# Four reorderings in a two-layer transformer step: query loads, weight splits and the first steps of a layer change places

## The chip, the cores and the metric

The kernel runs on one core of one Trainium2 chip. Its five engines work side by side, each through its own instructions in order: PE (matmuls), DVE, ACT, POOL and SP, which here only issues transfers. The metric is the time of one execution in microseconds (us), as the median of several runs.

## The reference

A step of a streaming encoder: 1024 prompt tokens and 64 sample tokens (1088 rows of 1024) go through two layers. All arithmetic is in float32.

```python
# layer 0: 8 latent heads (keys and values from a compressed latent, with a rotary part)
#          and 8 band heads (own chunk and 8 before, learned bias) side by side
y = concat([o_a, o_b]) @ w_out
x = LN(alpha * x + y);  x = LN(alpha * x + sqrelu_mlp(x))
# layer 1: 16 stick-breaking heads
w = where(mask, exp(log_sigmoid(z) + tail), 0);  o = w @ v
x = LN(alpha * x + o @ w_out);  x = LN(alpha * x + sqrelu_mlp(x))
```

Keys, values and latents of the new tokens are outputs too.

## The kernel before, in words

**Split products.** Each float32 operand is split into a high part (ACT, L148) and a low part (DVE, L149); a product is three matmuls, high x high, low x high, high x low (L153, L154, L155). So every weight, every activation and every softmax tile passes through ACT and DVE before PE can use it. `weight` (L179) loads a weight by SP and splits it.

**Order.** The program is written as steps, and a scheduler that models the engines puts each engine's instructions in an order. The kernel steers it with `after` and `paced`: a mark says "this instruction is to be ordered after that one". A mark makes no wait on the chip; it only moves an instruction in its engine's queue. Waits come from data and from buffers that are reused. SP can have at most eight transfers outstanding: the ninth waits for the first.

**Layer 0.** (1) `latents` projects the latents. (2) The queries (L466 `nope`, L474 `rotate`): query weights `u..` times the normed latents; the results are written to DRAM as `qm_d` and `qr_d` through four `raw` buffers, with constants `qc` beside them. (3) Band heads in four pairs (`heads64`), then (4) latent heads in four pairs (`proj_mla`, L934). While a pair is attended (`attend`: scores, softmax on DVE, ACT and POOL, transposes `t`, products `pv` with the values, result `o` written to `oT_d`), the steps that project the next pair are strewn between its units by `paced`. `attend` gives back a mark for each unit. In front of the latent heads stand the values of all latent heads (`vals`, 11 blocks) and the first pair's keys; the keys' shared rotary half is copied to a second set of buffers (`k0H`.., L930 to L932), and a part of the values too (`V`, L970). Each pair loads its queries from `qm_d` and `qr_d` (L943, L944).

**The end of each layer's mixer.** In the last pair, `out_early` (L1055) loads the eight blocks of the output weights (`in_w_out`), splits them (`wo_2`, `wo_3`, `wo_4` and so on are raw, high and low) and starts the output projection for the tokens that are already complete (EARLY), with PE free between the units. `out_proj` (L1117) does the rest, with an operand load (`oT_d`) and a residual load (`in_x` or `x_d`) for each block of tokens, and the layer norm.

**Layer 1.** After the MLP of layer 0, `finish` normalises each block of tokens, and `to_x` (L202) transposes and splits it as x for layer 1. `heads64` makes steps "k, q, v" each in three chunks of tokens (CHUNKS); for the first pair they run in the order k0 k1 k2 q0 q1 q2 v0 v1 v2.

Tile names in the rows below end in a number, which differs between two builds for the same tile.

Of the kernel before, what the change touches and what calls it, by code (L numbers as in the profile page):

```python
# [7 lines left out]
F32 = mybir.dt.float32  # L8
# [5 lines left out]
P = 128  # L14
# [37 lines left out]
def pieces(n):  # L52
    if n <= 512:
# [8 lines left out]
        [(0, 0), (1, 1), (0, 1), (1, 2), (0, 4), (1, 3), (0, 2), (0, 3), (1, 0)]]  # L62

# [56 lines left out]
class Net:  # L120
# [26 lines left out]
    def split(self, H, L, src, engine=None):  # L147
        self.nc.scalar.activation(H, src, AF.Copy)  # L148
        (engine or self.nc.vector).tensor_tensor(L, src, H.bitcast(F32), op=ALU.subtract)  # L149
# [29 lines left out]
    def weight(self, src, shape, mark=None):  # L179
# [10 lines left out]
        self.split(tiles[1], tiles[2], tiles[0])  # L190
# [11 lines left out]
    def to_x(self, y, rows):  # L202

        n = sum(r[1] for r in rows)
        for h in range(2):
            tp = self.ps("t", (P, 4, P))
            for j in range(4):
                c = (4 * h + j) * P
                self.transpose(tp[:, j, :n], y[:n, c : c + P])
            for t0, m, r in rows:  # L210
                s = (slice(None), slice(None), slice(t0, t0 + m))
                self.split(self.xH.tiles[h][s], self.xL.tiles[h][s], tp[:, :, r : r + m])

# [240 lines left out]
    def queries(self, qn, uw):  # L454
# [46 lines left out]
        late = None  # L501
        for m in range(4):
            for c in range(3):
                i = nope(m, c)
                late = late or i
            if m == 0:
                first = self.weight(io["w_bk"][0], [P, KD, P], late)
        for c0, n in CHUNKS:
            qc = self.tl(up, [ROPE, 384], "qc", 2)
            self.after(nc.sync.dma_start(qc[:, :n], io["qconst"][:, c0 : c0 + n]), late)  # L510
# [48 lines left out]
    def heads64(self, cp, bp, tiles, pair, w, cacheT, cache_v, outs, out0, cache_outs=(None, None), first=None, sooner=None):  # L559
# [57 lines left out]
        steps = [lambda a=a: step(*a) for a in ((kind, c0, n) for kind in "kqv" for c0, n in CHUNKS)]  # L617
# [197 lines left out]
    def even_mixer(self):  # L815
# [105 lines left out]
        self.paced(vals[:8], marks[1:])  # L921
# [8 lines left out]
        for e, half in ((0, slice(64, 128)), (1, slice(0, 64))):  # L930
            for a, b in zip(*(k[e] for k in ksets)):
                nc.sync.dma_start(b[half].bitcast(F32), a[half].bitcast(F32))  # L932

# [33 lines left out]
        self.paced(steps + vals[8:], None)  # L967

        Vs.append(self.tl(vb, [P, 11, 2, P], "V", 1, F32R))
        nc.sync.dma_start(Vs[1].bitcast(F32), Vs[0][:, :, 6:].bitcast(F32))  # L970
        for pair in range(4):
# [9 lines left out]
            marks = self.attend(cp, heads, row, 0)  # L981
            if pair == 3:
                ws, ys, steps = self.out_early(0, io["w_out0"], io["x"])
# [804 lines left out]
```

## Time and profile before

| | |
|---|---|
| median of 3 runs | 2856.91 us (2856.05 to 2858.45) |
| profiled execution | 2852.04 us |
| its span (first to last instruction) | 2850.3 us |
| mean granted clock of PE | 0.985 |
| idle time of PE in the span | 118.1 us |

A wait is named by the engine, the tile and line that wait, and the engine, tile and line waited for. The granted clock is that of PE, as a share of full speed. The DMA share is the mean busy share of the 16 DMA engines. Rows of SP ("SPq") are the issue of a transfer, not its run.

### The profile page before, as it was taken

How to read it: one execution, taken by the hardware profiler on the slowest of the kernel's cores; microseconds unless marked ns; L12 is line 12 of the kernel's file. 1: busy time of each engine (PE TensorE's matmuls, PEld its weight loads, DVE VectorE, ACT ScalarE, POOL GpSimd, SP SyncE). 2: the span in 40 equal slices, each digit the busy share in tenths (PEclk: the TensorE clock that was granted, in tenths of full speed). 3: DMA queues.
4: the chain of work that ended last, by engine and by line, in shares of the span. 5: the costliest groups of instructions: out<-in, count | busy, mean ns of one | idle time of the engine just before them, and what ended most of it. 6: DMA issues, size and time to landing. Idle time of an engine off the chain costs nothing.

```text
span 2850.3 us, 46910 instructions
## 1 busy us (share of the span) xinstructions
PE 2732.2 (96%) x16907; PEld 2497.7 (88%) x16907; DVE 2154.3 (76%) x3827; ACT 1511.9 (53%) x3104; POOL 767.9 (27%) x888
## 2 busy tenths in 40 slices
PE   8999996999999999999999999999899999999998
PEld 7989995887899998888789999998789999977886
DVE  4336675884877777999967888878777777789998
ACT  4226674883555555433257777777545555543331
POOL 3113332652300002222443433434330000122235
PEclk9999998999999999999999999999999999999999
DMA  6162234334234357443321111112252443654432
GB/s 196 33 188 67 70 99 105 75 109 118 93 132 152 129 167 262 122 153 118 123 82 60 50 52 50 61 52 69 87 160 90 153 146 133 232 179 130 157 120 78
DMA packets 228680, 331.47 MB, mean 116 GB/s; under 512 B 44736, under 2 KB 161120, under 8 KB 228448
## 3 DMA queue, kind: packets, MB, share of 16 engines
q1 hardware_dynamic: 228448, 328.48, 36.4%
q8 instruction: 134, 2.20, 0.3%
q14 instruction: 98, 0.80, 0.1%
HBM read 214.49 MB, written 109.99 MB: 114 GB/s over the span
## 4 chain that ended last, share of the span: by engine, by line
PE 74%; DVE 10%; ACT 5%; DMA 4%; issue 4%; POOL 2%; SPq 1%; DVEq 0%; ACTq 0%; POOLq 0%
PE d L153 9%; PE d L154 8%; PE d L155 8%; PE t L153 5%; PE t L155 5%; PE t L154 5%; PE s L153 5%; PE s L155 5%; PE s L154 5%; PE t L171 4%; PE s L642 3%; PE pv L776 2%; PE pv L774 2%; PE pv L155 2%; PE pv L153 2%
## 5 line engine op out<-in xcount | busy, mean ns | idle before, releaser
L710 POOL TENSOR_TENSOR G<-G,S 128x384 f32<-128x384 f32 (+4 forms) x200 | 204.1, 1024 | 346.3 <-DVE S L707 121.4
L153 PE MATMUL d<-xH,wH 128*128 128x384 f32 (+1 forms) x784 | 262.5, 335 | 3.0 <-ACT qS L599 2.2
L155 PE MATMUL d<-xH,wL 128*128 128x384 f32 (+1 forms) x784 | 262.3, 335 | 0.0
L154 PE MATMUL d<-xL,wH 128*128 128x384 f32 (+1 forms) x784 | 260.2, 332 | 0.0
L149 DVE TENSOR_TENSOR wtL<-t,wtH 128x512 fp32r<-128x512 f32 (+2 forms) x328 | 197.4, 619 | 54.4 <-ACT wtH L148 43.5
L148 ACT ACTIVATE wtH<-t 128x512 fp32r<-128x512 f32 (+2 forms) x328 | 170.1, 545 | 55.1 <-PE pv L774 24.3
L148 ACT ACTIVATE wo<-wo 128x1024 fp32r<-128x1024 f32 (+4 forms) x109 | 95.8, 887 | 156.7 <-DMA wo<-a_d 24.8
L774 PE MATMUL pv<-wtH,V 128*128 128x256 f32 (+1 forms) x624 | 159.7, 282 | 9.7 <-DVE o L738 6.6
L649 POOL TENSOR_TENSOR R<-R,inv 128x640 f32<-128x640 f32 (+6 forms) x100 | 116.1, 1173 | 186.9 <-DVE inv L648 132.4
L776 PE MATMUL pv<-wtL,V 128*128 128x256 f32 (+1 forms) x624 | 154.9, 290 | 9.7 <-DVE wtL L149 9.6
L707 DVE TENSOR_TENSOR_SCAN S<-S,own 128x513 f32<-128x513 f32 (+3 forms) x144 | 145.9, 1023 | 10.8 <-ACT S L700 9.0
L153 PEld LDWEIGHTS d<-xH,wH 128*128 128x128 f32 x784 | 148.2, 189 | 6.6 <-ACT qS L599 3.2
L155 PEld LDWEIGHTS d<-xH,wL 128*128 128x128 f32 x784 | 148.1, 189 | 1.2
L154 PEld LDWEIGHTS d<-xL,wH 128*128 128x128 f32 x784 | 148.1, 189 | 1.1
L776 PEld LDWEIGHTS pv<-wtL,V 128*128 128x128 f32 x624 | 121.0, 194 | 13.9 <-DVE wtL L149 12.6
L774 PEld LDWEIGHTS pv<-wtH,V 128*128 128x128 f32 x624 | 120.6, 193 | 14.0 <-DVE o L738 5.7
L171 PE MATMUL t<-ident,G 128*128 128x128 f32 x600 | 105.1, 281 | 15.9 <-POOL S L698 8.1
L149 DVE TENSOR_TENSOR wo<-wo,wo 128x1024 fp32r<-128x1024 f32 (+4 forms) x80 | 94.2, 1184 | 24.4 <-ACT wo L148 24.0
L642 PE MATMUL s<-kS,qH 128*128 128x384 f32 (+3 forms) x288 | 105.8, 369 | 3.6 <-DVE mx L665 1.8
L700 ACT ACTIVATE S<-s 128x384 f32<-128x384 f32 (+4 forms) x200 | 98.9, 494 | 17.6 <-PE s L642 15.4
L701 ACT ACTIVATE G<-s 128x384 f32<-128x384 f32 (+4 forms) x200 | 99.7, 499 | 0.1
L642 PE MATMUL s<-kS,qL 128*128 128x384 f32 (+3 forms) x288 | 96.8, 339 | 0.0
(1819 smaller groups left out, 9819.3 us busy)
## 6 DMA issues: line engine op xcount, KB each, us to landing
wo<-a_d SPq DMA_DIRECT2D x59, 512.0 KB, 3.9
wo<-in_w_dn SPq DMA_DIRECT2D x30, 512.0 KB, 5.7
a_d<-wo SPq DMA_DIRECT2D x27, 544.0 KB, 3.7
a_d<-sl SPq DMA_DIRECT2D x23, 544.0 KB, 3.4
sl<-in_w_up SPq DMA_DIRECT2D x22, 512.0 KB, 4.6
sl<-a_d SPq DMA_DIRECT2D x21, 512.0 KB, 3.9
sl<-in_w_dn SPq DMA_DIRECT2D x19, 512.0 KB, 5.0
xs<-a_d SPq DMA_DIRECT2D x19, 512.0 KB, 3.8
```

The costliest lines, as they stand in the source:

```text
L148: self.nc.scalar.activation(H, src, AF.Copy)
L149: (engine or self.nc.vector).tensor_tensor(L, src, H.bitcast(F32), op=ALU.subtract)
L153: i = mm(out, aH, bH, start=first, stop=False)
L154: mm(out, aH, bL, start=False, stop=False)
L155: mm(out, aL, bH, start=False, stop=last)
L171: return self.nc.tensor.transpose(out, in_, self.ident[:n, :n])
L642: self.nc.tensor.matmul(ps[:, :n], q, k, start=i == 0, stop=i == len(passes) - 1)
L649: nc.gpsimd.tensor_tensor(R[:, :nk], R[:, :nk], inv.to_broadcast([P, nk]), op=ALU.mult)
L707: nc.vector.tensor_tensor_scan(s[r], s[r], own, carry, op0=ALU.mult, op1=ALU.max)
L710: nc.gpsimd.tensor_tensor(G[:, :n], G[:, :n], S[:, 1 : n + 1], op=ALU.mult)
L774: mm(out, v, wH[:, s : s + n], start=bi == 0 and s == 0, stop=False)
L776: mm(out, v, wL[:, s - n : s], start=False, stop=bi == len(banks) - 1 and j == bank[-1][0])
```

## The change

It has four parts.

1. *Queries.* In the query phase, the load of the first band key weight is marked after the fifth `nope` block and its split after the ninth; the constants after the third; what followed `late` follows the tenth.
2. *Latent heads.* The copies of the keys and values move behind marks of the first latent pair's units; six instead of eight value blocks are strewn through the last band pair, the others and the first pair's key steps are marked after its last unit.
3. *Weight splits.* In `out_early` each split gets a mark of a unit of the last pair, by the table WEIGHTS. In `out_proj` the residual of the first block of tokens takes another buffer, and the layer norm's constants are loaded after the first product.
4. *Start of layer 1.* The first pair's steps run k0 q0 k1 q1 k2 q2 v0 v1 v2, and the transposes of the last two blocks of tokens are marked after steps 1 and 2.

```diff
+WEIGHTS = [[0, 1, 1, 2, 2, 3, 3, 5], [0, 0, 1, 1, 2, 2, 2, 5]]
...
-    def split(self, H, L, src, engine=None):
-        self.nc.scalar.activation(H, src, AF.Copy)
+    def split(self, H, L, src, engine=None, mark=None):
+        self.after(self.nc.scalar.activation(H, src, AF.Copy), mark)
...
-        self.split(tiles[1], tiles[2], tiles[0])
+        self.split(tiles[1], tiles[2], tiles[0], mark=ready)
...
-        late = None
-        for m in range(4):
-            for c in range(3):
-                i = nope(m, c)
-                late = late or i
-            if m == 0:
-                first = self.weight(io["w_bk"][0], [P, KD, P], late)
+        marks = [nope(m, c) for m in range(4) for c in range(3)]
+        late = marks[9]
+        first = self.weight(io["w_bk"][0], [P, KD, P], marks[4], marks[8])
         for c0, n in CHUNKS:
             qc = self.tl(up, [ROPE, 384], "qc", 2)
-            self.after(nc.sync.dma_start(qc[:, :n], io["qconst"][:, c0 : c0 + n]), late)
+            self.after(nc.sync.dma_start(qc[:, :n], io["qconst"][:, c0 : c0 + n]), marks[2])
...
-        self.paced(vals[:8], marks[1:])
+        self.paced(vals[:6], marks[1:])
...
-        self.paced(steps + vals[8:], None)
-        Vs.append(self.tl(vb, [P, 11, 2, P], "V", 1, F32R))
-        nc.sync.dma_start(Vs[1].bitcast(F32), Vs[0][:, :, 6:].bitcast(F32))
+        self.paced(steps + vals[6:], marks[-1:], 0)
+        def copies(marks):
+            for e, half in ((0, slice(64, 128)), (1, slice(0, 64))):
+                for a, b in zip(*(k[e] for k in ksets)):
+                    self.after(nc.sync.dma_start(b[half].bitcast(F32), a[half].bitcast(F32)), marks[1 + e])
+            Vs.append(self.tl(vb, [P, 11, 2, P], "V", 1, F32R))
+            self.after(nc.sync.dma_start(Vs[1].bitcast(F32), Vs[0][:, :, 6:].bitcast(F32)), marks[7])
...
+            if pair == 0:
+                copies(marks)
...
-                                io["cache_skT"], io["cache_sv"], {"k": io["o_skT"], "v": io["o_svT"]}, 0)
+                                io["cache_skT"], io["cache_sv"], {"k": io["o_skT"], "v": io["o_svT"]}, 0,
+                                order=None if pair else (0, 3, 1, 4, 2, 5, 6, 7, 8))
         score, V, steps = proj(0)
-        self.paced(steps, None)
+        firsts = [st() for st in steps]
+        for t, i in zip(self.turned[-2:], (1, 2)):
+            self.after(t, firsts[i])
...
-        for k in blocks + [self.late]:
+        for k, i in zip(blocks + [self.late], WEIGHTS[layer]):
...
-            self.split(*ws[k], raw)
+            self.split(*ws[k], raw, mark=marks[i])
...
-        loads, ops = {}, {order[0]: (*self.ahead[:2], self.out_residual(order[0], xres))}
+        loads, ops = {}, {order[0]: (*self.ahead[:2], self.out_residual(order[0], xres, 1))}
...
-        gb = [self.bcast(sl, io[f"ln_mix_{x}"][layer : layer + 1, :], D) for x in "gb"]
+        gb = []
...
+                        if not gb:
+                            gb = [self.bcast(sl, io[f"ln_mix_{x}"][layer : layer + 1, :], D, mark=first) for x in "gb"]
```

What that makes of the queues at three places. First SP, between the last band pair and the first latent pair (`oT_d<-o` are output writes, `V<-V` and `k..<-k..` the copies, `q` and `qS` the query loads), before:

```order
L779 DMA oT_d<-o_5387 64x256
L1063 DMA wH_2102_8409<-in_w_out 128x1024
L970 DMA V_5730<-V_5011 128x11x256
L779 DMA oT_d<-o_5430 64x256
L779 DMA oT_d<-o_5506 64x256
L932 DMA k0H_5650<-k0H_4985 64x1344
L932 DMA k0L_5651<-k0L_4986 64x1344
L779 DMA oT_d<-o_5562 64x256
L932 DMA k1H_5652<-k1H_4987 64x1344
L932 DMA k1L_5653<-k1L_4988 64x1344
L943 DMA q_5660<-qr_d 64x2x1024
L944 DMA qS_5658<-qr_d 64x2x64
```

and with the change:

```order
L784 DMA oT_d<-o_5387 64x256
L784 DMA oT_d<-o_5430 64x256
L784 DMA oT_d<-o_5506 64x256
L944 DMA q_5638<-qr_d 64x2x1024
L945 DMA qS_5636<-qr_d 64x2x64
L784 DMA oT_d<-o_5562 64x256
L944 DMA q_5638<-qm_d 64x2x1024
```

The loads of the first pair's queries now stand among the last output writes; the copies follow some twenty rows later.

Second PE, at the start of layer 1 (`s_16515` is the first key chunk, `t_16390` and `t_16399` turn block 8, the 64 sample tokens, `t_16452` block 7, the last to be normalised), before:

```order
L171 MATMUL t_16342<-ident_58,wo_15_2787_13545 128x128 x4
L153 MATMUL s_16515<-xH_3272_15950,wH_3370_16504 128x384
L154 MATMUL s_16515<-xL_3274_15952,wH_3370_16504 128x384
L155 MATMUL s_16515<-xH_3272_15950,wL_3371_16505 128x384
L171 MATMUL t_16390<-ident_58,wo_16_2789_13547 128x64 x4
L171 MATMUL t_16399<-ident_58,wo_16_2789_13547 128x64 x4
L171 MATMUL t_16452<-ident_58,sl_2_2788_13546 128x128 x4
```

and with the change (`d_16553`, the first query chunk, has 24 matmuls, of which the first and the last are shown):

```order
L155 MATMUL s_16515<-xH_3272_15950,wH_3370_16504 128x384
L156 MATMUL s_16515<-xL_3274_15952,wH_3370_16504 128x384
L157 MATMUL s_16515<-xH_3272_15950,wL_3371_16505 128x384
L155 MATMUL d_16553<-xH_3271_15949,wH_3376_16548 128x384
...
L157 MATMUL d_16553<-xH_3272_15950,wL_3377_16549 128x384
L173 MATMUL t_16390<-ident_58,wo_12_2789_13547 128x64 x4
L173 MATMUL t_16399<-ident_58,wo_12_2789_13547 128x64 x4
L155 MATMUL s_16584<-xH_3271_15949,wH_3370_16504 128x384
L173 MATMUL t_16452<-ident_58,wo_16_2788_13546 128x128 x4
```

A whole query chunk now stands ahead of the transposes of the last two blocks.

Third DVE, in the last pair of layer 1 (`S` are steps of the stick-breaking weights, `wtL` low parts of turned weights, `wL_4895`, `wo_4`, `wo_7` low parts of output weights), before:

```order
L149 TENSOR_TENSOR wL_4895_23800<-wL_4893_23797,wH_4894_23799 128x1024
L707 SCALAR_TENSOR_TENSOR S_23220<-S_23220,own_16473 128x385
...
L707 SCALAR_TENSOR_TENSOR S_23280<-S_23280,own_16473 128x513
L149 TENSOR_TENSOR wo_4_4874_23758<-wo_2_4872_23755,wo_3_4873_23757 128x1024
L149 TENSOR_TENSOR V_16489<-t_23147,V_16489 64x2x64
L149 TENSOR_TENSOR wo_7_4877_23764<-wo_5_4875_23761,wo_6_4876_23763 128x1024
L707 SCALAR_TENSOR_TENSOR S_23320<-S_23320,own_16473 128x385
L738 TENSOR_TENSOR o_23216<-pv_23203,o_23216 64x256
L149 TENSOR_TENSOR wtL_23247<-t_23241,wtH_23246 128x512
```

and with the change:

```order
L151 TENSOR_TENSOR V_16489<-t_23079,V_16489 128x6x64
L712 SCALAR_TENSOR_TENSOR S_23220<-S_23220,own_16473 128x385
...
L712 SCALAR_TENSOR_TENSOR S_23280<-S_23280,own_16473 128x513
L151 TENSOR_TENSOR V_16489<-t_23147,V_16489 64x2x64
L151 TENSOR_TENSOR wo_4_4874_23758<-wo_2_4872_23755,wo_3_4873_23757 128x1024
L151 TENSOR_TENSOR wtL_23247<-t_23241,wtH_23246 128x512
L712 SCALAR_TENSOR_TENSOR S_23320<-S_23320,own_16473 128x385
L743 TENSOR_TENSOR o_23216<-pv_23203,o_23216 64x256
L151 TENSOR_TENSOR wtL_23259<-t_23254,wtH_23258 128x384
L151 TENSOR_TENSOR wo_7_4877_23764<-wo_5_4875_23761,wo_6_4876_23763 128x1024
```

The split `wL_4895` has left the piece, and `V`, `o` and `wtL` stand ahead of the splits that they stood behind.

More of the change, by code (lines that the diff above doesn't have):

```diff
@@ L204, in to_x @@
         n = sum(r[1] for r in rows)
+        first = None
         for h in range(2):
@@ L615, in step @@
             return mark
-        steps = [lambda a=a: step(*a) for a in ((kind, c0, n) for kind in "kqv" for c0, n in CHUNKS)]
+        work = [(kind, c0, n) for kind in "kqv" for c0, n in CHUNKS]
+        if order:
+            work = [work[i] for i in order]
+        steps = [lambda a=a: step(*a) for a in work]
         def score(h, i):
```

28 lines of the change are left out of this document (14 added, 14 removed).

## The prediction

> **What bounds the kernel now.** I read the page's busy shares first, then the waits of PE, then the granted clock in windows around the longest of them, and last the timeline of the engine or queue that each wait names.
>
> ```profile
> PE 2732.2 (96%) x16907; PEld 2497.7 (88%) x16907; DVE 2154.3 (76%) x3827; ACT 1511.9 (53%) x3104; POOL 767.9 (27%) x888
> ```
>
> PE is busy for 2732.2 of 2850.3 us, and the change takes no matmul away. What it can win is idle time of PE, 118 us in all, and time in which PE runs at a lower clock. The waits (us in total, times, longest) that belong to the places it touches:
>
> ```profile
> PE s L642 <- DMA q<-qm_d: 15.0, 2, 14.6
> PE s L153 <- DVE raw L149: 6.4, 2, 5.2
> PE t L171 <- POOL wo L300: 4.9, 2, 4.5
> ```
>
> The clock around them, in windows (busy time of PE, PEld, DVE, ACT, POOL, then granted clock, DMA share, GB/s):
>
> ```profile
> 158.00:166.00 8.00, 5.12 (x17) 5.12 (x18) 1.86 (x3) 2.01 (x3) 0.00 (x0) 0.57 0.43 149
> 466.00:470.00 4.00, 1.97 (x8) 1.78 (x8) 1.53 (x4) 1.00 (x3) 0.00 (x0) 0.50 0.78 212
> 470.00:484.00 14.00, 0.01 (x1) 0.04 (x1) 0.25 (x1) 0.00 (x0) 0.00 (x0) 0.50 0.99 205
> 484.00:490.00 6.00, 5.65 (x16) 4.28 (x16) 3.01 (x10) 1.13 (x2) 0.00 (x0) 0.52 1.06 202
> 694.00:698.00 4.00, 4.00 (x11) 3.00 (x12) 4.00 (x6) 1.64 (x2) 0.00 (x0) 0.57 0.93 301
> 1468.00:1476.00 8.00, 4.01 (x18) 3.71 (x19) 6.63 (x10) 1.49 (x5) 6.03 (x10) 0.58 0.37 116
> 1990.00:2014.00 24.00, 14.24 (x58) 11.68 (x59) 23.95 (x29) 19.42 (x38) 17.26 (x19) 0.68 0.76 268
> ```
>
> The clock is 1.00 or 0.50, so a mean c says that (1 - c) / 0.5 of the stretch was at half, and half of PE's busy time in it is lost. Every long wait so costs twice: once as idle time, once in the slow matmuls behind it.
>
> **Place 1, the queries (about 155 to 166).** Issue rows of SP:
>
> ```profile
> 145.06 1.25 SPq L189 DMA_DIRECT2D wraw<-in_w_bk  x1
> 146.91 1.23 SPq L510 DMA_DIRECT2D qc<-in_qconst  x1
> ...
> 154.75 1.06 ACT L148 ACTIVATE wH<-wraw 128x1024 fp32r<-128x1024 f32 x1 [9.99 <-DMA wraw<-in_w_bk]
> ```
>
> ACT stands 9.99 us at the split of the first key weights, and the query blocks that PE waits for (5.2) are queued behind it. The change puts load and split behind the queries. That alone frees ACT at once. But the four `raw` buffers of the queries come free only when their `qr_d` writes have landed, so the wait does not vanish: what it gains is what leaves SP and the queues ahead of those writes, 1.25 + 1.23 = 2.5 us. The low clock lost (0.43/0.5) x 5.12 / 2 = 2.2 us there; with the stall halved I take half back, 1.1. Together **3.6**; ends 2 (the writes set it alone) and 7.4 (all of 5.2 and 2.2). The moved loads have nothing ahead of them but query work, and the band projections that need them come after all of the query blocks: nothing.
>
> **Place 2, from the band heads to the latent heads (461 to 490), the largest term.** PE and SP there:
>
> ```profile
> 463.11 0.39 PE L774 MATMUL pv<-wtH,V 128*128 128x256 f32 x1 [1.22 <-DVE o L738]
> 467.42 0.58 PE L774 MATMUL pv<-wtH,V 128*128 128x256 f32 x1 [2.70 <-DVE o L738]
> 483.99 0.66 PE L642 MATMUL s<-k0H,q 128*128 128x384 f32 x1 [14.60 <-DMA q<-qm_d]
> ...
> 461.99 0.65 SPq L970 DMA_DIRECT2D V<-V  x1
> 470.62 1.06 SPq L779 DMA_DIRECT2D oT_d<-o  x1
> 471.73 1.74 SPq L932 DMA_DIRECT2D k1H<-k1H  x1
> 477.05 0.61 SPq L943 DMA_DIRECT2D q<-qm_d  x1
> ```
>
> The copy of the values and the four of the keys go out ahead of the queries, and the DMA engines are full (0.99) all through the wait. In the change the queries stand directly behind the last output writes, the copies behind the queries of three pairs. Also, key and value blocks that were done before now stand between the last three `pv` groups, where PE waited 1.22 and 2.70. So: PE ended its work at 469.4; without 3.9 us of waits and the 1.0 us that the half clock cost from 466 to 470 it ends at 464.5. The last write of `o` goes out two value blocks (3 us) earlier plus the 1.24 us that it took from the last `pv` (469.38 to 470.62), at 462.7, and `q<-qm_d` one issue (1.06) later, at 463.8; I add 1 us because the softmax of the last units may hold `pv` back. A 512 KB load took
>
> ```profile
> wH<-in_w_out SPq DMA_DIRECT2D x1, 512.0 KB, 3.6
> ```
>
> 3.6 us with the queues nearly empty and 6.9 (477.05 to 483.99) behind the copies; here one 512 KB load is ahead, so 5.2. PE starts at 470.0 instead of 484.0: **14.0**. Some 5 us of idling are left, so the clock will still be at half afterwards, and I book nothing there (484 to 490 lost 2.7). Ends: 8 (queries as slow as in the full queues) and 17.
>
> The Trainium skill ("TensorE: Matmul & The Clock Gate", Part 1 and the closing table) says that the clock falls after a whole window of about 3.4 us without work and returns after one busy window. The trace doesn't fully agree: the clock was 0.50 from 466 on, after waits of 1.22 and 2.70 with work between. By its rule the short wait left at place 1 would cost no clock, and the sum would be 1.1 us better.
>
> The copies themselves now start behind the `qS` loads of the third pair:
>
> ```profile
> 496.19 0.51 SPq L944 DMA_DIRECT2D qS<-qr_d  x1
> ...
> k1L<-k1L SPq DMA_DIRECT2D x1, 336.0 KB, 4.8
> ...
> 515.83 0.34 PE L642 MATMUL s<-k0H,q 128*128 128x384 f32 x1
> ```
>
> All of this moves up by 14: issue from 484.6, landed by 492, first needed (the second pair's scores) at 501.8. Spare: 9.8 us, so nothing.
>
> **Place 3, last latent pair of layer 0 (618 to 645).**
>
> ```profile
> 617.60 1.03 SPq L1063 DMA_DIRECT2D wo<-in_w_out  x2
> ...
> 622.00:624.00 2.00, 1.85 (x14) 1.60 (x12) 2.00 (x6) 2.00 (x4) 1.68 (x1) 1.00 0.98 356
> ...
> 631.01 0.58 PE L776 MATMUL pv<-wtL,V 128*128 128x256 f32 x1 [2.54 <-DVE wtL L149]
> 635.72 0.58 PE L774 MATMUL pv<-wtH,V 128*128 128x256 f32 x1 [1.33 <-ACT o L734]
> ```
>
> The split of the last weight block leaves DVE's queue ahead of the `wtL` that PE waits 2.54 for: 1.2 better. But the first of the six weight loads, until now alone and earlier, goes out at 617.6 with the other five. At 356 GB/s one more 512 KB delays them all by 1.4 us, and ACT takes them in order. Another split (1.1) enters ACT's row ahead of the `o` at which PE waits 1.33. Later by 1.4 + 1.1 = 2.5, and the first `pv` 1.4. I take **-2.0**; ends -5 and +1.
>
> **Place 4, output projection of layer 0 (684 to 698).** The operand that PE waits for is the third operand load, behind four residuals:
>
> ```profile
> 678.64 0.50 SPq L1095 DMA_DIRECT2D xs<-oT_d  x1
> ...
> 684.11 0.38 SPq L1095 DMA_DIRECT2D wH<-oT_d  x1
> ...
> 688.43 0.58 ACT L148 ACTIVATE xs<-xs 128x448 fp32r<-128x448 f32 x1 [2.32 <-DMA xs<-oT_d]
> ...
> 693.84 0.50 PE L153 MATMUL d<-wo,xs 128*128 128x512 f32 x1 [3.65 <-ACT xs L148]
> ```
>
> It now goes out at the second's place, 678.6, whose data was there by 688.4 even behind other loads; PE asks at 693.84 - 3.65 = 690.2. The wait goes and the half clock from 694 (0.43/0.5 x 4.00 / 2 = 1.7) with it: 5.3; the residual loads that move behind could be late for some of it, so **5.0**, ends 2 and 5.4.
>
> **Place 5, start of layer 1 (1461 to 1476).** PE waits 4.5 for the layer norm of block 8, the 64 sample tokens, on POOL. The 24 matmuls of the first query chunk now stand there. The same block later took
>
> ```profile
> 1487.41:1491.74 4.33, 4.33 (x27) 4.33 (x27) 3.34 (x6) 2.60 (x8) 0.00 (x0) 1.00 0.42 135
> ```
>
> 4.33 us, which fills the wait. The clock lost (0.42/0.5) x 4.01 / 2 = 1.7. Together **6.0**; ends 4 and 6.7. Its weights are loaded and split long before. The work that filled later time is only exchanged, and behind it the matmuls of all three kinds are at hand.
>
> **Place 6, last pair of layer 1 (1986 to 2022).** Waits of PE in 1985 to 2015, a DVE row, POOL rows:
>
> ```profile
> PE t L171 <- POOL G L710: 4.8, 2, 3.4
> PE t L171 <- DVE V L149: 1.5, 1, 1.5
> PE pv L774 <- DVE o L738: 1.5, 1, 1.5
> ...
> 1987.25 1.22 DVE L149 TENSOR_TENSOR wL<-wL,wH 128x1024 fp32r<-128x1024 f32 x1 [0.41 <-ACT wH L148]
> ...
> 1998.92 0.87 POOL L710 TENSOR_TENSOR G<-G,S 128x384 f32<-128x384 f32 x1 [1.97 <-ACT wo L148]
> ...
> 2004.65 6.34 POOL L710 TENSOR_TENSOR G<-G,S 128x384 f32<-128x384 f32 x2 [0.95 <-ACT wraw L148]
> ```
>
> DVE is busy 23.95 of 24 us: here it is the bound. In the change one split (1.22) leaves this stretch altogether, and two others stand behind `V` and `o` instead of ahead of them. The two waits of 1.5 go, and of the 4.8 the first, 4.8 - 3.4 = 1.4: **4.4**. The splits still have to be done before the projection that fills PE afterwards, so 3.4 stays, and I book no clock. Ends 0 and 9 (all, with the (0.32/0.5) x 14.24 / 2 = 4.6 of clock).
>
> **Sum.** 3.6 + 14.0 - 2.0 + 5.0 + 6.0 + 4.4 = 31.0 us. The profiled execution took 2852.04, so 2821.0. The median of the runs, 2856.91, lies 4.9 above it, and goes to **2825.9**. All low ends together are +11 (2846), all high ends +46 (2811).
>
> **Rivals.**
> - *The splits hold the last pairs as before.* Two POOL adds took 6.34 us among the splits and one 0.87 outside them. If the adds, not DVE's order, set place 6, its 4.4 are gone, and place 3 is at its -5: 31.0 - 4.4 - 3.0 = 23.6, **2833**. For it: DVE has no free time to give. Against: 1.22 really leaves. The Trainium skill ("SBUF — State Buffer", two separate sides) has GpSimd locked out for the whole of a DVE instruction with two SBUF inputs; by that rule this rival holds, since the change only reorders such splits. The 6.34 agrees in direction.
> - *The transfers set the start of the latent heads.* Four query loads (2 MB) at 205 GB/s are 10.2 us; if they all end together, PE starts at 463.8 + 1 + 10.2 = 475: place 2 gives 9, **2831**. For it: 0.99 DMA share; against: issue order, and 3.6 us for the same size.
> - *The change doesn't do what it says.* The marks set an order, not a wait; if the loads' landings and not their places decide, places 1, 2 and 4 give little, and the result is within 0.2% (5.7 us, about what a measurement of this kernel can tell), **2853**. Against: the copies are plainly ahead of the queries in the rows above.
> - *The copies are late (slower).* They wait behind a `qS` load, which needs a buffer that POOL clears when the first pair's loads have landed. Each us beyond the spare 9.8 stops the second pair's scores. From 9.8 + 31.0 + 5.7 = 46.5 us late, that is landing after 538, the kernel is slower by over 0.2%: **2863** or more. For it: POOL clears in its own order; against: in the rows above those loads went at 496, right behind the first scores.
>
> **How the numbers follow.** Forecast 0.57, first rival 0.22, second 0.11: all faster, 0.90. No effect 0.06, slower 0.04. The range 2811 to 2846 is that of the ends summed above; it holds the first three cases but for a tenth of them, which is 0.8.
>
> **What would show it.** Right: the wait for `q<-qm_d` falls from 14.6 to about 5; 4.5 for `wo L300` and 3.65 for `xs` go; `raw L149` falls to about 2.7; at 612 to 645 ACT waits for `in_w_out`; in 1986 to 2014 DVE stays full but `V` and `o` leave the list. Wrong: `q<-qm_d` still above 8; a new wait for `k0H<-k0H`; the half clock at the same length in place 6 with `POOL G` grown by what `V` and `o` lost.

## The result, and the profile after

The changed kernel took a median of 2838.66 us (four runs, 2836.11 to 2843.75) against 2856.48 us of the kernel before on the same chip (four runs, 2854.91 to 2858.45). The ratio is 0.9939 [0.9922, 0.9957], a gain of 17.8 us. Forecast were 31.0 us, to 2825.9 (2811 to 2846): the kernel is faster, but by 13 us less. In a later comparison (five runs against nine) the ratio was 0.9947 [0.9934, 0.9959], 14.6 us.

The page of after, and from its list of PE's waits (us in total, times, longest) those of the places named before and the new ones:

```profile
PE 2740.8 (96%) x16907; PEld 2500.9 (88%) x16907; DVE 2162.8 (76%) x3827; ACT 1512.6 (53%) x3104; POOL 762.5 (27%) x888
```

```profile
PE s L155 <- DVE raw L151: 4.7, 1, 4.7
PE s L647 <- DMA q<-qm_d: 4.3, 1, 4.3
PE t L173 <- POOL sl L305: 2.3, 2, 1.4
PE d L155 <- DVE sl L1173: 2.3, 1, 2.3
PE t L173 <- POOL wo L305: 1.9, 3, 1.2
PE d L155 <- ACT sl L150: 1.6, 1, 1.6
```

The wait for the latent queries fell from 14.6 to 4.3, those for `xs` (3.65) and `wo` (4.5) are gone, that for `raw` only went from 5.2 to 4.7. The three rows for `sl` belong to the output projection of layer 1, on which the prediction said nothing. PE's idle time fell from 118.1 to 101.2 us (span 2842.0 less 2740.8), but PE was *busy* 8.6 us longer with the same 16907 matmuls.

The granted clock accounts for 5.3 us of that: PE's busy time at half speed rose from 47.9 to 58.5 us. The other 3.3 us are not explained. In windows of after (PE, PEld, DVE, ACT, POOL busy, clock, DMA share, GB/s) around the start of the latent heads, and three in the projection:

```profile
431.52:438.35 6.83, 6.12 (x21) 4.93 (x20) 4.22 (x16) 3.79 (x9) 2.41 (x3) 0.50 0.10 22
452.00:455.42 3.42, 2.83 (x14) 2.74 (x14) 0.78 (x3) 1.24 (x5) 3.27 (x5) 0.50 0.06 10
476.94:482.72 5.78, 5.44 (x14) 4.08 (x14) 2.94 (x9) 1.13 (x2) 0.70 (x1) 0.50 1.06 201
2069.92:2073.33 3.41, 3.41 (x9) 2.65 (x9) 3.41 (x6) 0.95 (x1) 0.00 (x0) 0.50 0.90 350
2127.95:2131.36 3.41, 3.41 (x16) 3.41 (x17) 3.41 (x7) 0.00 (x0) 0.00 (x0) 0.50 0.02 5
2145.01:2148.43 3.42, 3.35 (x16) 3.36 (x16) 3.05 (x3) 3.42 (x6) 0.01 (x1) 0.50 0.38 153
```

and the same two places of the projection in before:

```profile
2066.00:2080.00 14.00, 14.00 (x65) 11.58 (x64) 5.35 (x10) 1.94 (x5) 0.00 (x0) 1.00 0.71 219
2130.00:2150.00 20.00, 18.83 (x128) 17.51 (x128) 19.39 (x29) 6.85 (x14) 2.62 (x3) 1.00 0.16 53
```

Before the change the whole projection ran at full speed; after it, three stretches of 3.41 us ran at half.

Where the time went is seen by matching each matmul of after with the same one of before (same output, operands and turn) and taking the median shift near a point. The table gives the change over each stretch, in us, for two profiled executions of after (spans 2842.0 and 2838.7), and for a second one of before (span 2851.2), all against the first of before (2850.3), in its times. Two columns split the change of the first profile of after: idle time of PE, and half of PE's busy time at half clock; what is left is in neither.

| stretch of before | forecast | after, 1st | of it idle | of it half clock | after, 2nd | before, 2nd |
|---|---|---|---|---|---|---|
| 100 to 230, place 1 (queries) | -3.6 | -1.3 | -1.2 | +0.3 | -1.1 | -0.9 |
| 230 to 300 | 0 | +1.6 | 0.0 | +1.7 | +1.6 | 0.0 |
| 400 to 520, place 2 (latent heads) | -14.0 | -7.2 | -11.4 | +3.5 | -7.2 | -0.6 |
| 570 to 665, place 3 (last pair, layer 0) | +2.0 | +1.1 | -0.8 | +0.6 | +1.1 | +1.9 |
| 665 to 720, place 4 (projection, layer 0) | -5.0 | -4.0 | -2.5 | -1.7 | -5.0 | +0.1 |
| 720 to 1440 | 0 | -0.7 | -0.7 | 0.0 | -2.5 | +0.3 |
| 1440 to 1520, place 5 (start of layer 1) | -6.0 | -4.6 | -3.4 | -2.1 | -4.6 | +0.2 |
| 1970 to 2040, place 6 (last pair, layer 1) | -4.4 | -3.5 | -0.7 | -2.0 | -3.4 | -0.1 |
| 2040 to 2200 (projection, layer 1) | 0 | +10.1 | +3.7 | +5.1 | +9.5 | 0.0 |

The first profile of after is 8.3 us shorter than that of before, where 31.0 were forecast. Two terms make up 17 us of this gap: place 2 gave half, and 10 us were lost where nothing was forecast. The profiles differ by 8.3 and 12.5 us and the medians by 17.8 and 14.6. Both profiled executions of before lie below its median (all its runs beside the experiments: 2847.6 to 2863.6), so some us of the medians' gain are in executions without a profile, and are not located.

### The profile page after: what moved, and what is told of

Same layout as the page of the kernel before. It is cut to its first block, busy times and chain, and to the rows that moved or that the text cites. A ratio compares the mean times of both kernels' runs of the same rounds, so it can differ in the third digit from the quotient of the medians.

```text
span 2842.0 us, 46908 instructions
## 1 busy us (share of the span) xinstructions
PE 2740.8 (96%) x16907; PEld 2500.9 (88%) x16907; DVE 2162.8 (76%) x3827; ACT 1512.6 (53%) x3104; POOL 762.5 (27%) x888
## 4 chain that ended last, share of the span: by engine, by line
PE 77%; DVE 8%; ACT 5%; DMA 4%; issue 3%; POOL 2%; SPq 0%; DVEq 0%; ACTq 0%; POOLq 0%
PE d L155 9%; PE d L157 9%; PE d L156 9%; PE t L155 5%; PE t L156 5%; PE t L157 5%; PE s L155 5%; PE s L156 5%; PE s L157 5%; PE t L173 4%; PE s L647 3%; PE pv L781 2%; PE pv L779 2%; PE pv L157 2%; PE pv L155 2%
## 5 line engine op out<-in xcount | busy, mean ns | idle before, releaser
L150 ACT ACTIVATE wtH<-t 128x512 fp32r<-128x512 f32 (+2 forms) x328 | 170.3, 545 | 53.8 <-PE pv L779 26.8
L150 ACT ACTIVATE wo<-wo 128x1024 fp32r<-128x1024 f32 (+3 forms) x106 | 92.5, 880 | 156.6 <-DMA wo<-a_d 23.2
L781 PEld LDWEIGHTS pv<-wtL,V 128*128 128x128 f32 x624 | 120.2, 193 | 12.4 <-DVE wtL L151 10.7
L647 PE MATMUL s<-kS,qH 128*128 128x384 f32 (+3 forms) x288 | 105.6, 368 | 3.8 <-DVE mx L670 2.3
L151 DVE TENSOR_TENSOR wo<-wo,wo 128x1024 fp32r<-128x1024 f32 (+4 forms) x76 | 92.7, 1227 | 20.7 <-ACT wo L150 20.5
```

The lines of the kernel that those rows point to most:

```text
L150: self.after(self.nc.scalar.activation(H, src, AF.Copy), mark)
L647: self.nc.tensor.matmul(ps[:, :n], q, k, start=i == 0, stop=i == len(passes) - 1)
L781: mm(out, v, wL[:, s - n : s], start=False, stop=bi == len(banks) - 1 and j == bank[-1][0])
```

## The experiments

All but the second profile of before and the kernel with added waits were timed against before on the same chip; the chips differ between groups of kernels, so a kernel is compared with one of another group by the ratio. PE idle is the span less PE's busy time; "at half" is PE's busy time in the stretches granted at 0.50, both of the profiled execution.

| kernel | median us (runs) | ratio to before | PE idle | at half |
|---|---|---|---|---|
| before, first and second profile | | | 118.1, 117.6 | 47.9, 49.5 |
| after | 2838.66 (4) | 0.9939 [0.9922, 0.9957] | 101.2 | 58.5 |
| after again | 2840.44 (5) | 0.9947 [0.9934, 0.9959] | 97.3 | 61.5 |
| blocks back | 2840.12 (5) | 0.9945 [0.9933, 0.9958] | 105.6 | 40.2 |
| third block first | 2837.30 (5) | 0.9937 [0.9925, 0.9950] | 98.1 | 51.3 |
| queries first | 2832.97 (5) | 0.9921 [0.9908, 0.9935] | 93.7 | 57.4 |
| both orders | 2830.78 (4) | 0.9917 [0.9900, 0.9934] | 92.7 | 50.6 |
| both orders, blocks back | 2831.87 (5) | 0.9919 [0.9902, 0.9936] | 99.9 | 47.4 |
| splits of layer 1 as before | 2834.15 (6) | 0.9931 [0.9914, 0.9948] | 98.3 | 44.4 |
| the same, queries first | 2837.79 (6) | 0.9925 [0.9913, 0.9938] | 97.2 | 53.4 |
| splits of layer 0 as before | 2847.30 (6) | 0.9961 [0.9949, 0.9973] | 105.2 | 68.1 |
| start of layer 1 as before | 2844.86 (6) | 0.9949 [0.9936, 0.9962] | 103.4 | 52.0 |

In all of them, and in the last experiment too, the busy time less half of the part at half speed is 2708 to 2713 us (2708.2 and 2708.9 in before, 2710.1 to 2713.2 in the others). So the span is this floor, plus the idle time, plus half of the slow busy time: a forecast has these two parts to get right above all. What moves the floor by up to 5 us is not shown.

**Second profiles of after and of before.**

> The changed kernel once more, for a second profile. Theory A (where a half-speed stretch falls is luck of the execution: the same short waits cost one in one execution and none in the next): of the fourteen half-speed stretches of the first profile some are gone or moved, those behind waits of under 2.3 us (at 243.8, 1114.2, 2127.95, 2500.0) first; the waits themselves keep their lengths within 0.3 us; PE's busy sum at half speed is 48 to 58 us, and the profile's time is 2836 to 2840. Theory B (each stretch follows from the waits ahead of it): the same fourteen at the same places within 1 us, and a time of 2842 to 2845.

> The kernel before once more, for a second profile. Theory A (the clock is set in windows of 3.41 us that run through: a window with more than about 1.7 us without PE work makes the next one slow, so the same waits cost a slow window or none by where they fall): PE's matmuls come at the same distances as in the first profile but for steps of about 1.7 us where a slow window is there in one and not in the other; waits of 1.2 to 2.7 us are where they differ. Theory B (executions differ evenly): the distance grows little by little over the span.

After: the slow stretches stood at the same places, except that the one at 1114 was gone and one at 25 had come. Their sum was 61.5, outside the 48 to 58 of theory A, and the time, 2840.44, just above its 2836 to 2840. Theory B is out by the missing one: a wait for `wo` of 2.07 at 1111 in the first execution was followed by a slow stretch, one of 1.80 there in the second was not, and the second did 2.2 us better. But most of the slow stretches are not luck; they came again. Before: the shift changed in steps (+1.6 between 570 and 610, where the same wait of 1.58 was followed by a slow stretch in this execution alone) and was nearly level between, as A has it. But at that step A's reason does not hold: the window ahead of the slow one held 1.0 us of idling, and in the first execution a window there with 1.5 was followed by none.

**Place 2: the queries ahead of the last writes.** The last three writes of the band heads' outputs are ordered behind the first pair's query loads:

```diff
+        self.outs.append(self.nc.sync.dma_start(dst[r : r + 64, c0 : c0 + 2 * P], o))
...
+        last = self.outs[-3:]
...
+        for o, i in zip(last, (1, 1, 3)):
+            self.after(o, self.qloads[i])
```

> The changed kernel, with the last three writes of the band heads' outputs put behind the first pair's query loads in SP's row. Theory A (the query load's place behind those writes, which wait for the last products, holds the latent heads): q<-qm_d is issued 2 to 4 us sooner, the wait of 4.3 for it falls under 1, the half clock from 475.9 goes, and the kernel is 4 to 7 us faster than the changed one. Theory B (the transfer, not the issue, sets it: 512 KB in queues full of copies): the load only takes longer, the wait stays at 3 to 4.3, and the time is the same within 1.5 us.

SP's row in after, and then in this kernel (start and length of the issue in us; its lines are one number higher):

```profile
467.90 0.45 SPq L784 DMA_DIRECT2D oT_d<-o  x1
468.45 0.55 SPq L944 DMA_DIRECT2D q<-qr_d  x1
469.10 0.55 SPq L945 DMA_DIRECT2D qS<-qr_d  x1
470.74 0.48 SPq L784 DMA_DIRECT2D oT_d<-o  x1
471.27 0.59 SPq L944 DMA_DIRECT2D q<-qm_d  x1
```

```profile
459.68 1.21 SPq L945 DMA_DIRECT2D q<-qr_d  x1
460.98 0.55 SPq L946 DMA_DIRECT2D qS<-qr_d  x1
461.59 0.59 SPq L945 DMA_DIRECT2D q<-qm_d  x1
464.92 4.87 SPq L785 DMA_DIRECT2D oT_d<-o  x2
```

and PE, first in after, then here:

```profile
472.26 0.39 PE L157 MATMUL d<-wH,ckL 128*64 128x512 f32 x1
476.94 0.66 PE L647 MATMUL s<-k0H,q 128*128 128x384 f32 x1 [4.29 <-DMA q<-qm_d]
```

```profile
473.67 0.39 PE L158 MATMUL d<-wH,ckL 128*64 128x512 f32 x1
473.90 0.34 PE L648 MATMUL s<-k0H,q 128*128 128x384 f32 x1
...
478.51 0.30 PE L648 MATMUL s<-k1H,q 128*128 128x128 f32 x1 [1.83 <-DVE nm L691]
```

`q<-qm_d` goes out 9.7 us sooner (more than the 2 to 4 expected, since nothing before it waits for the last products) and the wait is gone, with a new one of 1.83 behind it, which has a slow stretch behind it in turn (from 479.6), where A had none. Otherwise theory A: the runs (2830.66 to 2835.50) do not touch those of after (2837.21 to 2842.47); the medians differ by 7.5 us. In its profile it gains 4.0 us more than after in this stretch, and loses some 2 less in the projection of layer 1. So the place of that load in SP's row, and not the transfer, held the start.

**Place 2: the blocks of values and keys back.**

```diff
-        self.paced(vals[:6], marks[1:])
+        self.paced(vals[:8], marks[1:])
...
-        self.paced(steps + vals[6:], marks[-1:], 0)
+        self.paced(steps + vals[8:], None)
```

> Of part 2 only the order of loads is kept (queries ahead of the copies); the blocks of keys and values that the change lets stand among the last band heads go back to where they stood before (eight blocks of values strewn over the band heads, the rest in one row behind them). Theory A (those blocks fill waits for the last softmaxes): the waits of 1.2 and 2.7 behind the last DVE products come back, PE ends its band work 1 to 3 us later, the wait for the first queries is about as long as in the changed kernel (4 to 5), and the kernel is 1 to 4 us slower than the changed one. Theory B (the blocks only push the last units back, and the last writes and the query load with them): PE starts on the latent heads 1 to 2 us sooner and the kernel is 1 to 3 us faster than the changed one.

Its waits of PE between 460 and 485:

```profile
PE s L647 <- DMA q<-qm_d: 8.1, 2, 7.4
PE pv L779 <- DVE o L743: 2.4, 2, 1.2
```

Both theories were half right. The waits for `o` came back (A), and PE still ended its band work sooner (469.4 against 472.7), as the slow stretches at 431 and 452 were gone; between 400 and 520 this profile won 2.1 us more than after (B). The time is that of after: whatever PE saved it spent in a longer wait for the queries, as their load hung on the last writes as before. With both loads reordered *and* the blocks back:

> The kernel of both reorderings, with the blocks of keys and values among the last band heads put back as before the change. Theory A (the blocks only held the band heads back, and with the queries there in time that is what is left of the wait): no wait for q<-qm_d above 1 us, no slow windows from 430 to 460, waits of 1.2 and 1.2 for o, and 1 to 4 us faster than with the blocks among the heads. Theory B (the blocks fill waits that are there whatever the queries do): 1 to 3 us slower than with them, by the waits of 1.2 and 2.7 for o.

A is out: the wait for `q<-qm_d` was still 3.1 us, and a slow stretch of 6.8 us stood at 432. The median is 1.1 us above that with the blocks among the heads (2831.87 against 2830.78, same chip), which would be B's, but lies inside the spread of the runs. Where the blocks stand is worth nothing that could be measured.

**Layer 1's projection: the third block's loads first.** Behind the change, the operand and residual loads of the third block of tokens stand behind gain, bias and two others in SP's row. In this kernel they go ahead:

```diff
-        loads[t] = self.out_load(t, xres)
+        loads[t] = self.out_load(t, xres, head[0] if head else None)
...
-        gb = [self.bcast(sl, io[f"ln_mix_{x}"][...], D, mark=first) for x in "gb"]
+        gb = [self.bcast(sl, io[f"ln_mix_{x}"][...], D, mark=head[0] if head else first) for x in "gb"]
```

> The changed kernel, with the operand and residual loads of the third token block of layer 1's output projection ahead of the gain and bias and the other loads in SP's row, where the changed kernel has them behind. Theory A (the loss at 2066 comes from that load's place in the row, 12.4 us from issue to landing): the waits of 1.55 and 0.40 at 2066.7 and the 1.7 us of half clock behind them are gone, and the kernel is 2 to 4 us faster than the changed one. Theory B (DVE or POOL bound the projection, and PE that came early only waits later): the wait at 2066.7 goes and comes back between 2080 and 2150 as longer waits for DVE's or POOL's sl; the time is that of the changed kernel within 1 us.

PE in after, and PE's waits from 2060 to 2160 in this kernel:

```profile
2068.28 0.50 PE L155 MATMUL d<-wo,sl 128*128 128x512 f32 x1 [1.55 <-ACT sl L150]
...
2127.80 0.49 PE L155 MATMUL d<-wo,wo 128*128 128x272 f32 x1 [2.25 <-DVE sl L1173]
...
2142.57 1.09 PE L173 MATMUL t<-ident,sl 128*128 128x128 f32 x8 [0.93 <-POOL sl L305]
2145.08 0.47 PE L173 MATMUL t<-ident,sl 128*128 128x128 f32 x1 [1.41 <-POOL sl L305]
```

```profile
PE t L173 <- POOL sl L305: 3.6, 2, 1.9
PE t L173 <- POOL wo L305: 0.6, 1, 0.6
```

The wait at 2066 is gone, and instead of 2.25 and 0.93 + 1.41 there are 1.94 and 1.70, with one slow stretch instead of three. In the profile the projection loses 5.1 us where after loses 10.1 and 9.5; the medians differ by 3.1 us, with overlapping runs. Theory A by its number, though B's "comes back later" is in it: DVE and POOL still hold PE for 3.6 us. How much the loads' order is worth is not shown by this alone: in four other kernels (queries first, the same with layer 1's splits as before, layer 0's splits as before, start of layer 1 as before) that keep after's order, the wait for `ACT sl` is missing too, and they lose 4 to 8 us here.

> The changed kernel with both reorderings of SP's row: the first pair's query loads ahead of the last three output writes, and in layer 1's output projection the third block's operand and residual loads ahead of gain, bias and the rest. Theory A (the two losses are independent): the gains add, 7.5 and 3.1 us, and the time is 2828 to 2832. Theory B (the second gain was where the waits fell among the clock's windows): the time is that of the first reordering alone, 2831 to 2834, with slow windows in the projection again.

2830.78 (2828.50 to 2832.66) is in A's range, but the gains of 7.5 and 3.1 do not add up: by the ratios (0.9917 against 0.9921) it is 1 us better than the queries alone, which the intervals do not part. Slow windows are in the projection again (6.8 us from 2106.8), as B has it. That is nearer to B. This kernel has the lowest median and ratio of all, 23.7 us below before on its chip, and its interval [0.9900, 0.9934] touches that of after's later comparison only at the edge.

**Place 6 and the projection: layer 1's splits as before.**

```diff
-            self.split(*ws[k], raw, mark=marks[i])
+            self.split(*ws[k], raw, mark=None if layer else marks[i])
```

> The changed kernel with the splits of layer 1's last weights in the order of before. Theory A (the marks took the split out of DVE's way): the waits for V and o (1.5 each) between 1985 and 2015 are back, and the kernel is 2 to 5 us slower than the changed one. Theory B (POOL's adds set this stretch, whatever DVE's order): the time is that of the changed kernel within 1.5 us. In both, if the loss in the output projection of layer 1 comes from the loads' order and not from the splits, the waits at 2066, 2125 and 2141 stay.

PE's waits from 1960 to 2160:

```profile
PE t L173 <- POOL G L715: 6.5, 2, 5.1
PE t L173 <- DVE V L151: 2.6, 1, 2.6
PE t L173 <- POOL sl L305: 1.7, 1, 1.7
PE d L155 <- DVE sl L1173: 1.2, 1, 1.2
```

The wait for `V` is back, and place 6 gave 1.2 to 1.6 us less than in after (by where the stretch is cut), as A has it. But the kernel was not slower: the projection's waits were again the 1.2 and 1.7 of before, none followed by a slow stretch, and it lost 2.0 to 2.5 us instead of 9.5. In total 2834.15, with an interval that overlaps after's. The waits at 2066, 2125 and 2141 were to stay if the loss came from the loads' order and not from the splits; with that order unchanged they shrank to 0.4, 1.2 and 1.7, so that order alone does not set them. The next kernel asked whether that was the marks' doing:

> The splits of layer 1's last weights in the order of before, and the first pair's query loads ahead of the last three output writes. Theory A (two independent losses; without the marks the projection's waits are 1.2 and 1.7, each too short for a slow window): no slow window between 2030 and 2200, no wait for q<-qm_d above 1, the gains of 7.5 and 5 add, and the time is 2825 to 2829. Theory B (the gain without the marks was luck of the clock's windows): slow windows in the projection are back, and the time is that of the queries' order alone, 2831 to 2834.

It was not the marks alone. With the queries first, the same splits gave 2.3 for `DVE sl` and 2.3 for `POOL sl` again, a slow stretch at 2140, and 0.9925 against 0.9921 for the queries alone. B. Which pair of waits the projection gets (1.2 and 1.7, or 2.3 and 2.3) follows from how DVE's and POOL's work of the layer norm falls there; what sets that is open. What it costs is not: the two waits of under 1.75 us cost their length, the others brought one or two slow stretches of 1.7 us each.

**Place 3: layer 0's splits as before.**

```diff
-            self.split(*ws[k], raw, mark=marks[i])
+            self.split(*ws[k], raw, mark=marks[i] if layer else None)
```

> The changed kernel with the splits of layer 0's last weights in the order of before; layer 1's stay as changed. Theory A (the prediction's step: the first of the six weight loads joins the other five and its split enters ACT's row, a loss of 2.0): the kernel is 1 to 3 us faster than the changed one, the difference between 610 and 645. Theory B (the split that leaves DVE's row is worth as much as the load costs): the time is the changed kernel's within 1 us.

Neither: by the ratios it is 4 to 6 us *slower* than after (the intervals overlap at their edges), so in the changed kernel the marks of layer 0 seem to be a gain. In the profile it loses 4.8 us against after between 570 and 665 (and 3 more at 490, behind a wait of 2.62 for `wtH` whose link to the edit was not shown). ACT and PE in before, ahead of the last pair:

```profile
595.91 1.05 ACT L148 ACTIVATE wH<-wraw 128x1024 fp32r<-128x1024 f32 x1
...
598.26 0.38 ACT L733 ACTIVATE otmp<-pv 64x256 f32<-64x256 f32 x1
598.67 0.38 ACT L734 ACTIVATE o<-pv 64x256 f32<-64x256 f32 x1
```

```profile
599.10 0.30 PE L791 MATMUL pv<-wtH,V 128*128 128x64 f32 x1 [1.58 <-ACT o L734]
```

The split of the first weights (1.05) stood in ACT's row shortly ahead of the `o` that PE waited 1.58 for. The change moves it away; undone, the wait is back (1.59 at 594.5), here with two slow stretches behind it.

**Place 5: the start of layer 1 as before.**

```diff
-                                order=None if pair else (0, 3, 1, 4, 2, 5, 6, 7, 8))
+                                order=None)
...
-        firsts = [st() for st in steps]
...
+        self.paced(steps, None)
```

> The changed kernel with the first steps of layer 1 in the order of before. Theory A (the matmuls of the first query chunk fill the wait for the layer norm of the sample tokens): PE waits 4 to 5 us for POOL's wo at 1460 again, two slow windows behind it, and the kernel is 4 to 6.5 us slower than the changed one. Theory B (the work is only exchanged, and the wait comes back in another place): within 1.5 us of the changed kernel.

PE's waits from 1450 to 1480, and the window behind:

```profile
PE t L173 <- POOL wo L305: 4.5, 1, 4.5
```

```profile
1458.30:1465.20 6.90, 3.50 (x16) 3.19 (x17) 6.02 (x10) 1.60 (x5) 3.25 (x2) 0.54 0.42 133
```

At the place A holds: wait and slow stretch are back and 4.6 us are lost. In the total (0.9949 against 0.9947 and 0.9939) less than that shows; in the profile the projection of layer 1 gave 3 to 4 us back, with one slow stretch there instead of three.

**What a wait costs: added waits.** In the up projection of layer 0 PE waits for nothing. Ahead of 22 products the weights pass through short DVE operations that leave their values as they are:

```diff
+        def stall(w, ps, n):
+            x = w[:, 0, 0, :]
+            nc.vector.scalar_tensor_tensor(x, ps[:, :P], 0.0, x.bitcast(F32), op0=ALU.mult, op1=ALU.add)
+            for _ in range(n):
+                nc.vector.tensor_scalar(x, x.bitcast(F32), 1.0, 0.0, op0=ALU.mult, op1=ALU.add)
...
+                    if not layer and not c and i in (2, 5) and 3 <= m < 14:
+                        stall(w, ps, STALLS[2 * (m - 3) + (i > 3)])
```

> The changed kernel with 22 waits put into the up projection of layer 0, where PE otherwise waits for nothing: ahead of 22 products the weights go through 1 to 17 short DVE operations (times one), so that PE stands about 0.8 us and 0.2 us more for each, 0.8 to 4 us. The order of PE is kept. Theory A (the clock of a window of 3.41 us on a fixed grid is half when PE stood for more than about half of the window before, 1.5 to 1.9 us): each window with more than 1.9 us of standing is followed by a slow one and none with less than 1.4; a wait of 2 to 3 us that is cut by the grid into two parts under 1.4 costs its length only. In time: the sum of the waits (45 to 50 us) and 1.7 us for each slow window, of which there are 8 to 14. Theory B (only a whole window without work slows the clock): no slow window here, and the time grows by the waits alone. Theory C (a wait over 2 us slows the clock wherever it falls): the grid does not matter, and waits of the same length all cost the same.

The slow stretches of every trace begin at whole multiples of 3.413 us from each other. Two of the added waits, 2.74 and 2.13 us:

```profile
852.36 0.36 PE L157 MATMUL t<-wo,wo 128*128 128x272 f32 x1 [2.74 <-DVE wo L1292]
...
979.96 0.37 PE L157 MATMUL t<-xs,wo 128*128 128x272 f32 x1 [2.13 <-DVE wo L1292]
```

and windows cut on that grid, three around the first and two around the second:

```profile
847.63:851.04 3.41, 1.99 (x16) 1.76 (x14) 2.91 (x9) 1.73 (x5) 0.00 (x0) 1.00 0.00 0
851.04:854.45 3.41, 2.09 (x17) 2.12 (x18) 1.35 (x6) 0.00 (x0) 0.00 (x0) 1.00 0.00 0
854.45:857.86 3.41, 3.41 (x30) 3.41 (x29) 1.70 (x4) 2.48 (x6) 0.00 (x0) 1.00 0.00 0
977.34:980.75 3.41, 1.28 (x10) 1.09 (x10) 2.16 (x9) 2.21 (x5) 0.00 (x0) 1.00 1.07 340
980.75:984.16 3.41, 3.41 (x17) 3.41 (x16) 2.54 (x5) 0.63 (x1) 0.00 (x0) 0.50 0.35 133
```

The longer wait lies across a border, 1.42 in one window and 1.32 in the next, and the clock stays at 1.00. The shorter one lies whole in a window, and the next window is at 0.50. So with all 22: 13 windows of the stretch had over 1.85 us idle at full clock, and each was followed by a slow one; none with less was, though waits of 2.39 and 2.48 are among those that were cut. Theory A with its count (8 to 14); B and C fall. The span grew by 112.8 us against the second profile of after (83.5 of idle time, 26.8 of half clock), more than expected: the waits came to 66.8 instead of 45 to 50, and fixing PE's order brought two more, 10.2 and 2.3 us, ahead of the stretch.

## Why the prediction was right and wrong

**Place 1, 3.6 forecast, about 1.2 measured, little more than two profiles of before differ.** The ten later kernels, which have the same order here, lie between 2.2 us won and 1.4 lost against the first profile of before, so no gain is shown. Two steps failed. "That alone frees ACT at once": ACT in after stands as long as before, now for the next query weights.

```profile
154.33 0.85 ACT L150 ACTIVATE u3H<-uraw 128x768 fp32r<-128x768 f32 x1 [9.72 <-DMA uraw<-in_w_uq]
...
159.03 0.49 ACT L150 ACTIVATE raw<-s 128x384 fp32r<-128x384 f32 x1 [3.14 <-DMA qr_d<-raw]
```

And "what leaves SP and the queues ahead of those writes, 1.25 + 1.23 = 2.5 us": ACT's split that waits for those writes came at 159.03 instead of 159.75, and PE's wait went from 5.2 to 4.7. The alternative end, "the writes set it alone", fits this, and with 4.7 us idle the half clock stayed too.

**Place 2, 14.0 forecast, 7.2 measured.** The mechanism was right: the copies had held the queries (with the loads' order alone, "blocks back", the stretch gives 9.3). The transfer was nearly right too: 5.67 us from issue (471.27) to use (476.94), forecast 5.2. The step that failed is the one ahead, "without 3.9 us of waits and the 1.0 us that the half clock cost from 466 to 470 it ends at 464.5". PE ended at 472.65, 8.2 us later, with the same 2809 matmuls done as in before. From 400 us up to there it stood 8.4 us against 9.5 in before, where 3.9 less were booked, and the half clock (the stretches at 431 and 452) cost 4.5 instead of 1.0, which was to go; 0.8 us are in neither. The waits for `o` shrank, but others came (0.79, 0.59, 0.60, 0.55, and 1.84 for `mx` where there was 0.45). With the blocks back, the wait for `mx` is 0.46 again and those for `o` are 1.2 to 1.3, so the place of the blocks trades one for the other; both slow stretches are gone there, but with both orders and the blocks back one stands at 432 again. The last write, and the query load tied to it, moved with PE's end. The "1 us because the softmax of the last units may hold pv back" was that term. The rival "the transfers set the start", whose 9 us for this place come nearer, has the wrong cause: with the load issued early the wait vanished.

**Place 3, a loss of 2.0 forecast, 1.1 measured; the sign of the part itself seems wrong.** Against the second profile of before the stretch won 0.8 us. Only the place to which the splits move was looked at, not the one that they leave (591 to 597), where 1.58 us were won. Against the kernel without this part the changed one is 4 to 6 us faster, with intervals that overlap.

**Places 4 and 5: 5.0 and 6.0 forecast; 4.0 to 5.0 and 4.6 measured.** The waits went as said. At place 5 the idle time fell by 3.4 us instead of 4.3, as short waits (0.7, 0.6, 0.3) remain. Place 4 had no run of its own; its cause rests on the wait that went.

**Place 6: 4.4 forecast, 3.4 to 3.5 measured, the number right in part by luck.** The waits for `V` and `o` went. PE's waits from 1970 to 2000 in after:

```profile
PE t L173 <- POOL G L715: 4.0, 3, 2.4
PE d L157 <- DVE wo L151: 2.6, 1, 2.6
PE t L173 <- POOL S L703: 2.6, 3, 1.7
```

`G` fell from 4.8 to 4.0, where 3.4 was forecast, and a wait of 2.6 (1.9 in the second profile) came for `wo`, a low part that DVE made right behind a weight split. So the idle time fell by 0.7 and 1.8 us in the two profiles, not by 4.4; the half clock gave 2.0 and 0.6, for which nothing was booked. The first rival, "the splits hold the last pairs as before", is nearer to this than the forecast's step.

**Not forecast: 10 us in the projection of layer 1.** No term followed what an earlier PE finds behind the places that the change touches. PE arrived there some 18 us earlier, the operand of the third block took 12.4 us to land (issued 2054.87; before, 6.4), and waits of 1.17 and 1.70 became 1.95, 2.25 and 2.34. That is 3.7 us of waiting and 5.1 us of half clock. None of the rivals had it. With the third block's loads first the loss was about 5 us, with layer 1's splits as before, at as early an arrival, about 2; what sets it stays open.

**The clock.** Some 5.5 us of the sum were booked for it (1.1, 1.0, 1.7 and 1.7 at places 1, 2, 4 and 5), as if it went with the wait. Some did, but the waits left or newly made were still long enough. PE's time at half went up, from 47.9 and 49.5 to 58.5 and 61.5: 11.3 us more, 5.6 lost.

## What to carry to other kernels

Where one engine is busy nearly throughout, write the span as a nearly fixed floor, plus idle time, plus half of the time at half clock, and forecast the last two apart. Idling of under 1.4 us in a clock window nearly always cost its length only; from 1.9 us in a single window on, it also cost up to 1.7 us of half clock; between the two it went either way. So bringing the idling of a window below that can win more than the waiting that it saves. When work moves, price the queue that it leaves as well as the one that it joins, and follow the transfer that everything hangs on back to what *it* waits for: a load behind a write of the last result starts only when that result is there.

## What the runs showed of the hardware

The slow clock comes in whole windows of 3.413 us on a grid that stays fixed through an execution. Over 14 traces from 60 us on, a window at full clock in which PE stood 1.9 us or more was followed by a slow one 128 times of 128; with 1.4 to 1.9 us, 35 times of 83; with less, 12 times of some 10,900 (nine of them at one place, 447 to 452, which is not explained). A slow window with more than 0.65 us idle was never followed by a full one. Since any shift ahead moves the program against the grid, the same waits can cost more or less: the pair of 0.49 and 1.62 us at 242 fell into one window in after and was followed by a slow one, which is the +1.6 between 230 and 300; in before a border cut it, and nothing followed.

The Trainium skill ("TensorE: Matmul & The Clock Gate", Part 1) states the free-running window of 3413 ns, and the traces agree. It has the clock fall after a whole idle window; here 2.13 us of idling in a window were enough, and where page and measurement differ the measurement decides.
